# First six up-projection units on six blocks of k, with two modulation groups moved

## The chip, the cores and the metric

One NeuronCore of a Trainium2 chip runs the whole program. The engines named below are TensorE (PE, matrix products; PEld is its weight load), VectorE (DVE), ScalarE (ACT) and SyncE (SP, which here issues nearly all loads). The metric is the device time of one execution in microseconds; three runs of the kernel before are given by their median.

## The reference

One layer of a hybrid decoder on x of 256 tokens by D = 2048, with a conditioning vector c of 2048. All in fp32:

```
mod = silu(c) @ w_ada + b_ada            # 6 rows of 2048: shift, scale, gate twice
h = rms_norm(x) * (1 + scale_m) + shift_m
proj = h @ w_in                          # attention heads and a state-space mixer from it
mix = concat(rms_norm(attn), ssm) @ w_out
x = x + gate_m * mix
h = rms_norm(x) * (1 + scale_f) + shift_f
u = causal_conv3(h @ w_up)               # w_up: 2048 x 11264
x = x + gate_f * ((silu(g) * val) @ w_down)   # g, val: the halves of u
return rms_norm(x)
```

The change concerns the end of the product with w_out, the second norm with its shift and scale, and the product with w_up.

## The kernel before

**Layout.** Features lie on the 128 partitions, tokens along the free axis, so x is 16 blocks (kt) of 128x256. A product goes over the 16 blocks of k. Every weight block is used three times (`mm3`): the rounded weights h times the rounded activations (L277), h times the activations' remainder (L278), and the weights' remainder l times the rounded activations (L279), each 128x128 by 128x256.

**A unit** is a load of mostly 1024 KB (128x2048 fp32, 16 blocks) into a slot of the weight pool. `load_unit` (L252) issues it on SP, `hi_lo_part` makes h by a cast on ACT (L258) and l by a subtraction on DVE (L259), in pieces of 1024 columns. There are four buffers each for h and l, three accumulators in PSUM, and three slots for the loads; during the second half of the out projection three further slots (`wsb`) exist, on memory that the mixer leaves (among it `sqa`, so the first loads into them wait for PE's `ssg`). A slot is free for the next load when the last subtraction (or modulation operation) has read it. SP issues its loads in order: one whose slot is taken holds back all behind it.

**Modulation.** `mod` is made in 24 groups of four units, 1024 KB each (L201). A group in `ON_PE` is done by PE: four products `adp` per unit (L217), and after the fourth unit a row copy on ACT (L221), four column products `adc` (L224) and two small copies on DVE. A group outside it is four DVE operations with an accumulated sum (L210). Groups 12 to 19 give shift and scale of the second norm, two blocks each: 12 to 15 for blocks 0 to 7, 16 to 19 for 8 to 15; 20 to 23 give the last gate.

**Order.** `ORDER` is a list of tokens that the builder follows: `O.h.i` is unit i of half h of the out projection, `ada.g.i` a modulation unit, `N` and `NG` the norm of the mixer's output. A scheduler then places the instructions on the engines; some tokens have a higher priority. The out projection takes first the attention's eight blocks (half 0, `cat`), then the state space's (half 1, `cats`). Between them the second normalisation of the mixer stands: DVE sums squares in `sqa`, PE adds them over the partitions (`ssg`, L623), ACT takes the root (`std_ssm`), DVE the reciprocal (`rs_ssm`, L300), and DVE multiplies (`sn`, L628); ACT rounds the product into `cats`, DVE makes its remainder (L308).

**The feed-forward part** starts with `stats`: PE adds the squares of x over the partitions (`ssx`, L604 to L606), then root and reciprocal (`rs_x`). `h2_gen(a, b)` norms the blocks a to b (per block DVE L312, ACT L313, DVE L314). The product with w_up has 44 pairs of columns; pairs 0 to 21 go in two passes: pass one, `u1a`, takes blocks 0 to 7 of k, one unit of 16 weight blocks for each pair, and is copied out as `part` (L777); pass two, `u2a`, takes blocks 8 to 15 and adds the part. The first two units of pass one (`lead`) are loaded, and the first half of each is split, before the norm is there. Between the units of pass one stand modulation units of groups 17 to 19 on DVE. `w_dn` and the other 22 pairs (`ua`) follow. Below, `s_`, `h_`, `l_` are the load, the rounded part and the remainder of a weight; `o` belongs to w_out, `u` to w_up, `d` to w_dn.

## Time and profile before

| what | value |
| --- | --- |
| three runs | 1196.82, 1199.82, 1199.87 us (median 1199.82) |
| the profiled execution | 1196.57 us, of which the profile's span is 1194.8 |
| PE busy | 1167.5 us, 98% of the span |
| DVE busy | 915.0 us, 77% |
| ACT busy | 636.9 us, 53% |
| out projection, second half | 405.44 to 454.0 us of the span |
| entry of the feed-forward part | 454.03 (first `ssx`) to 460.09 us (first up matmul) |
| up units 2 and 6 of pass one begin | 474.45 and 496.21 us |
| pass two begins | 583.25 us |

Times in the rows are counted from the span's start. A row of a timeline may hold several instructions that follow one another (x2, x3). What stands in brackets behind it is the idle time of the engine just before and what ended it. Neighbouring matmuls overlap, so a matmul costs less than the length of its row.

### The profile page before, as it was taken

How to read it: one execution, taken by the hardware profiler on the slowest of the kernel's cores; microseconds unless marked ns; L12 is line 12 of the kernel's file. 1: busy time of each engine (PE TensorE's matmuls, PEld its weight loads, DVE VectorE, ACT ScalarE, POOL GpSimd, SP SyncE). 2: the span in 40 equal slices, each digit the busy share in tenths (PEclk: the TensorE clock that was granted, in tenths of full speed). 3: DMA queues.
4: the chain of work that ended last, by engine and by line, in shares of the span. 5: the costliest groups of instructions: out<-in, count | busy, mean ns of one | idle time of the engine just before them, and what ended most of it. 6: DMA issues, size and time to landing. Idle time of an engine off the chain costs nothing.

```text
span 1194.8 us, 23406 instructions
## 1 busy us (share of the span) xinstructions
PE 1167.5 (98%) x9760; PEld 1113.3 (93%) x9760; DVE 915.0 (77%) x1371; ACT 636.9 (53%) x959; POOL 0.9 (0%) x7
## 2 busy tenths in 40 slices
PE   6999999999999999999999999999999999999996
PEld 3899989988878898999999999999999999999995
DVE  6889979987988798786599984446888889656554
ACT  4544434457786544446567654444555555555552
POOL 0000000000000000000000000000000000000000
PEclk8899999999999999999999999999999999999998
DMA  9989988776765996997565545558878776545552
GB/s 359 409 338 337 327 335 304 276 268 246 287 242 214 365 383 237 343 357 245 183 204 186 201 146 194 195 194 276 295 299 301 284 282 227 196 150 196 194 194 96
DMA packets 47444, 309.60 MB, mean 259 GB/s; under 512 B 5568, under 2 KB 6761, under 8 KB 16105
## 3 DMA queue, kind: packets, MB, share of 16 engines
q1 hardware_dynamic: 46170, 307.04, 70.6%
q8 instruction: 76, 1.25, 0.4%
q10 hardware_dynamic: 1168, 1.06, 0.4%
q14 instruction: 30, 0.25, 0.1%
HBM read 305.98 MB, written 2.11 MB: 258 GB/s over the span
## 4 chain that ended last, share of the span: by engine, by line
PE 96%; DVE 1%; DMA 1%; ACT 1%; SPq 0%; issue 0%; DVEq 0%; ACTq 0%
PE ua L278 7%; PE ua L279 7%; PE da L279 7%; PE da L278 7%; PE da L277 7%; PE ua L277 7%; PE wa L277 6%; PE wa L279 6%; PE wa L278 6%; PE va L348 4%; PE u1a L278 3%; PE u1a L279 3%; PE u1a L277 3%; PE u2a L277 3%; PE u2a L279 3%; PE u2a L278 3%
## 5 line engine op out<-in xcount | busy, mean ns | idle before, releaser
L258 ACT CAST h_u<-s_u 128x1024 fp32r<-128x1024 f32 x176 | 183.6, 1050 | 188.3 <-PE ua L278 95.2
L259 DVE TENSOR_TENSOR l_u<-s_u,h_u 128x1024 fp32r<-128x1024 f32 x176 | 213.4, 1223 | 66.6 <-ACT h_u L258 64.6
L277 PE MATMUL ua<-h,h_u 128*128 128x256 f32 x704 | 194.3, 276 | 0.0
L278 PE MATMUL ua<-h,h_u 128*128 128x256 f32 x704 | 194.3, 276 | 0.0
L279 PE MATMUL ua<-h,l_u 128*128 128x256 f32 x704 | 194.3, 276 | 0.0
L279 PE MATMUL da<-g,l_d 128*128 128x256 f32 x704 | 194.3, 276 | 0.0
L278 PE MATMUL da<-g,h_d 128*128 128x256 f32 x704 | 194.3, 276 | 0.0
L277 PE MATMUL da<-g,h_d 128*128 128x256 f32 x704 | 194.1, 276 | 0.0
L259 DVE TENSOR_TENSOR l_d<-s_d,h_d 128x1024 fp32r<-128x1024 f32 (+1 forms) x128 | 108.8, 888 | 83.6 <-ACT h_d L258 83.6
L277 PE MATMUL wa<-hT,h_w 128*128 128x256 f32 x576 | 162.1, 282 | 0.8 <-ACT h_w L258 0.8
L279 PE MATMUL wa<-hT,l_w 128*128 128x256 f32 x576 | 159.8, 279 | 0.0
L278 PE MATMUL wa<-hT,h_w 128*128 128x256 f32 x576 | 159.7, 278 | 0.0
L258 ACT CAST h_d<-s_d 128x1024 fp32r<-128x1024 f32 (+1 forms) x128 | 98.2, 782 | 115.0 <-PE da L278 104.3
L210 DVE SCALAR_TENSOR_TENSOR ada<-ada,cb 128x2048 f32<-128x2048 f32 x60 | 137.2, 2288 | 11.5 <-DMA ada<-w_ada 11.2
L279 PEld LDWEIGHTS da<-g,l_d 128*128 128x128 f32 x704 | 132.2, 188 | 0.0
L277 PEld LDWEIGHTS ua<-h,h_u 128*128 128x128 f32 x704 | 132.2, 188 | 0.0
L278 PEld LDWEIGHTS ua<-h,h_u 128*128 128x128 f32 x704 | 132.2, 188 | 0.0
L279 PEld LDWEIGHTS ua<-h,l_u 128*128 128x128 f32 x704 | 132.2, 188 | 0.0
L278 PEld LDWEIGHTS da<-g,h_d 128*128 128x128 f32 x704 | 132.2, 188 | 0.0
L277 PEld LDWEIGHTS da<-g,h_d 128*128 128x128 f32 x704 | 132.1, 188 | 0.0
L258 ACT CAST h_w<-s_w 128x1024 fp32r<-128x1024 f32 x72 | 73.7, 1048 | 88.3 <-PE wa L278 42.7
L277 PEld LDWEIGHTS wa<-hT,h_w 128*128 128x128 f32 x576 | 108.4, 188 | 11.3 <-ACT h_w L258 3.6
(236 smaller groups left out, 2689.4 us busy)
## 6 DMA issues: line engine op xcount, KB each, us to landing
ada<-w_ada SPq DMA_DIRECT2D x96, 1024.0 KB, 6.1
s_u<-w_up SPq DMA_DIRECT2D x88, 1024.0 KB, 5.0
s_d<-w_dn SPq DMA_DIRECT2D x64, 704.0 KB, 4.1
s_w<-w_in SPq DMA_DIRECT2D x36, 1024.0 KB, 7.1
s_o<-w_out SPq DMA_DIRECT2D x16, 1024.0 KB, 8.3
s_v<-w_vdt SPq DMA_DIRECT2D x8, 1040.0 KB, 6.6
x<-xT SPq DMA_DIRECT2D x4, 512.0 KB, 4.8
outT<-x SPq DMA_DIRECT2D x2, 640.0 KB, 3.0
```

The costliest lines, as they stand in the source:

```text
L210: dve.scalar_tensor_tensor(ws[:, :D], ws[:, :D], 1.0, cb, op0=ALU.mult, op1=ALU.mult, accum_out=mod[:, j:j + 1])
L258: act.copy(wh[:, :m], ws[:, o:o + m])
L259: dve.tensor_sub(wl[:, :m], ws[:, o:o + m], wh[:, :m].bitcast(F32))
L277: pe.matmul(o, whs, a[:, 0:T], start=first, stop=False)
L278: pe.matmul(o, whs, a[:, T:2 * T], start=False, stop=False)
L279: pe.matmul(o, wls, a[:, 0:T], start=False, stop=last)
L348: pe.matmul(va[tt][i][:, :n], lo if st == 2 else hi, (wl if st == 1 else wh)[:, s], start=f and st == 0, stop=l and st == 2)
```

## The change

`ON_PE` loses group 14, which so goes to DVE. Group 15 leaves `ORDER` and becomes the first entry of `ada_rest`, the list of the units that are done in pass one, ahead of groups 17 to 23. Since blocks 6 and 7 of the second norm need group 15, the first six pairs (`NEARLY`) take only blocks 0 to 5 of k in pass one, in units of 12 weight blocks (1536 columns, 768 KB), and blocks 6 to 15 in pass two, in two half units of 10 weight blocks (1280 columns, 640 KB) for each pair. The norm of blocks 0 to 5 is made first, that of 6 and 7 behind unit 3. The two lead units' second halves are split only after the sixth block of the norm on DVE (`issue_after`). Group 16 stays on PE ahead of the lead units. The count of up matmuls stays: 72 of them move from pass one to pass two.

```diff
-ON_PE = {2, 6, 9, 10, 11, 12, 13, 14, 16}
+ON_PE = {2, 6, 9, 10, 11, 12, 13, 16}
+
+NEARLY = 6
+UP1 = [[((j, 44 + j), _k)] for _k0, _j0, _j1 in ((6, 0, 6), (8, 6, 22)) for j in range(_j0, _j1) for _k in [tuple(range(_k0))]]
+UP2 = ([[((c,), tuple(range(6, 16)))] for j in range(6) for c in (j, 44 + j)]
+       + [[((j, 44 + j), tuple(range(8, 16)))] for j in range(6, 22)])
...
-O.1.0 O.1.1 ada.14.2 O.1.2 ada.14.3 O.1.3 ada.15.0 O.1.4 ada.15.1 ada.15.2 O.1.5 O.1.6 ada.15.3 O.1.7
+O.1.0 O.1.1 ada.14.2 O.1.2 ada.14.3 O.1.3 O.1.4 O.1.5 O.1.6 O.1.7
...
         dve.tensor_add(par[:, b:b + n], mod[:, b:b + n], V("b_ada", b, n))
         dve.scalar_tensor_tensor(par[:, b:b + n], par[:, b:b + n], 1.0, V(g, k0, n), op0=ALU.add, op1=ALU.mult)
 
-    ada_next = [[8, 0]]
+    ada_rest = [(g, i) for g in (15, 17, 18, 19, 20, 21, 22, 23) for i in range(4)]
 
     def ada_some(n, last=24):
         for _ in range(n):
-            g, i = ada_next[0]
-            if g < last:
-                ada_unit(g, i)
-                ada_next[0] = [g, i + 1] if i < 3 else [g + 1, 0]
+            if ada_rest and ada_rest[0][0] < last:
+                ada_unit(*ada_rest.pop(0))
 
 
     preloaded = []
...
-        dve.scalar_tensor_tensor(dst[:, T:2 * T], t, s, dst[:, 0:T].bitcast(F32), op0=ALU.add, op1=ALU.subtract)
+        return dve.scalar_tensor_tensor(dst[:, T:2 * T], t, s, dst[:, 0:T].bitcast(F32), op0=ALU.add, op1=ALU.subtract)
...
-        else:
-            ada_next[0] = [g, i + 1] if i < 3 else [g + 1, 0]
...
                 steps[it[0]](*it[1:])
         else:
             steps[it[0]](*it[1:])
+    def up1_src(j):
+        return w_up1a[j] if j < NEARLY else w_up1[j - NEARLY]
+
     for j in range(NLEAD):
-        preloaded.append(load_unit(w_up1[j], 2048, f"u1_{j}"))
+        preloaded.append(load_unit(up1_src(j), 1536, f"u1_{j}"))
     for i in range(4):
         ada_pre[16, i] = ada_load(16, i)
     lead_ws = [preloaded.pop(0) for j in range(NLEAD)]
-    lead_hl = [hi_lo_part(lead_ws[j], 0, 1024, f"u1_{j}") for j in range(NLEAD)]
+    lead_hl = [hi_lo_part(lead_ws[j], 0, 768, f"u1_{j}") for j in range(NLEAD)]
     mixctx.close()
     wst["pat"] = [0]
...
     def h2_gen(a, b):
         ada_params(3, a, b - a, "g_ffn")
         for kt in range(a, b):
-            ada_norm(h2[:, kt, :], kt, rs2, par[:, 64 + kt:65 + kt], par[:, 48 + kt:49 + kt], f"2_{kt}")
+            r = ada_norm(h2[:, kt, :], kt, rs2, par[:, 64 + kt:65 + kt], par[:, 48 + kt:49 + kt], f"2_{kt}")
+        return r
 
     hk = [h2[:, k, :] for k in range(KT)]
...
     def resid_add(i, o, gate):
         dve.scalar_tensor_tensor(x[:, i, :], o, gate, x[:, i, :], op0=ALU.mult, op1=ALU.add)
 
-    h2_gen(0, 8)
+    h2_last = h2_gen(0, 6)
     parts = []
     ws, hl = lead_ws, lead_hl
-    ada_some(4, 17)
+    for i in range(4):
+        ada_unit(16, i)
     lead = [acc_tile(f"u1a{j}") for j in range(NLEAD)]
-    for i in range(8):
+    for i in range(6):
         b = slice(i * P, i * P + P)
         for j in range(NLEAD):
-            mm3(lead[j][:, 0:T], hl[j][0][:, b], hl[j][1][:, b], hk[i], i == 0, i == 7)
+            mm3(lead[j][:, 0:T], hl[j][0][:, b], hl[j][1][:, b], hk[i], i == 0, i == 5)
     for j in range(NLEAD):
-        wh, wl = hi_lo_part(ws[j], 1024, 1024, f"u1_{j}")
-        for i in range(8):
+        with tc.issue_after(h2_last.ins):
+            wh, wl = hi_lo_part(ws[j], 768, 768, f"u1_{j}")
+        for i in range(6):
             b = slice(i * P, i * P + P)
-            mm3(lead[j][:, T:2 * T], wh[:, b], wl[:, b], hk[i], i == 0, i == 7)
+            mm3(lead[j][:, T:2 * T], wh[:, b], wl[:, b], hk[i], i == 0, i == 5)
     for j in range(NHALF):
         if j < NLEAD:
             acc = lead[j]
         else:
-            u = weight_unit(w_up1[j], 2048, f"u1_{j}")
+            n = 6 if j < NEARLY else 8
+            u = weight_unit(up1_src(j), 256 * n, f"u1_{j}")
             acc = acc_tile(f"u1a{j}")
-            gemm_pair(acc, u, 0, hk[:8])
+            gemm_pair(acc, u, 0, hk[:n])
         part = gp.tile([P, 512], F32, tag="g", name=f"part{j}")
         act.copy(part, acc)
         parts.append(part)
-        ada_some((16 * (j + 1)) // 18 - (16 * j) // 18, 20)
+        with tc.issue_after(h2_last.ins):
+            ada_some(1 if j < 4 else (12 * (j - 3)) // 16 - (12 * (j - 4)) // 16, 20)
+            if j == 3:
+                h2_gen(6, 8)
     ada_some(100, 20)
     h2_gen(8, 16)
     for half in range(2):
...
         for jj in range(NHALF):
             j = half * NHALF + jj
             if half == 0:
-                w = weight_unit(w_up1[NHALF + j], 2048, f"u2_{j}")
                 acc = acc_tile(f"u2a{j}")
-                gemm_pair(acc, w, 0, hk[8:])
+                if j < NEARLY:
+                    for s in range(2):
+                        w = weight_unit(w_up1b[2 * j + s], 1280, f"u2_{j}_{s}")
+                        gemm_part(acc[:, s * T:(s + 1) * T], w, hk[6:], True, True)
+                else:
+                    w = weight_unit(w_up1[16 + j - NEARLY], 2048, f"u2_{j}")
+                    gemm_pair(acc, w, 0, hk[8:])
                 dve.tensor_add(parts[j], parts[j], acc)
                 us = [parts[j][:, s * T:(s + 1) * T] for s in range(2)]
             else:
...
-    w_up1 = np.stack([unit([((j, 44 + j), _r(8 * h, 8 * h + 8))], wu) for h in range(2) for j in range(NHALF)])
+    w_up1a = np.stack([unit(e, wu) for e in UP1[:NEARLY]])
+    w_up1 = np.stack([unit(e, wu) for e in UP1[NEARLY:] + UP2[2 * NEARLY:]])
+    w_up1b = np.stack([unit(e, wu) for e in UP2[:2 * NEARLY]])
```

The order on DVE from the end of the first half of the out projection to the second's first weights, before (`l1024_o0_7` is the remainder of half 0's last unit, `sqs6` and `sqs7` the last squares):

```order
L259 TENSOR_TENSOR l1024_o0_7_4465<-s_o0_7_4458,h1024_o0_7_4464 128x1024
L617 TENSOR_TENSOR sqa_2378<-sqa_2378,sqs6_4377 128x256
L617 TENSOR_TENSOR sqa_2378<-sqa_2378,sqs7_4529 128x256
L651 TENSOR_TENSOR ot_3633<-ot_3633,rs_attn_3550 128x512
L652 TENSOR_TENSOR x_103<-x_103,ot_3633 128x512
L300 RECIPROCAL rs_ssm1_4542<-std_ssm1_4540 128x256
L628 SCALAR_TENSOR_TENSOR sn4_4544<-cxs_173,vec_92,rs_ssm1_4542 128x256
...
L628 SCALAR_TENSOR_TENSOR sn7_4556<-cxs_173,vec_92,rs_ssm1_4542 128x256
L308 TENSOR_TENSOR cats_4038<-sn4_4544,cats_4038 128x256
...
L308 TENSOR_TENSOR cats_4038<-sn6_4552,cats_4038 128x256
L259 TENSOR_TENSOR l0_o1_0_4568<-s_o1_0_4565,h0_o1_0_4567 128x1024
```

and now (`ada14_0` to `ada14_3` are the units of group 14):

```order
L263 TENSOR_TENSOR l1024_o0_7_4465<-s_o0_7_4458,h1024_o0_7_4464 128x1024
L621 TENSOR_TENSOR sqa_2378<-sqa_2378,sqs6_4377 128x256
L216 SCALAR_TENSOR_TENSOR ada14_0_4521,mod_99<-ada14_0_4521,cb_95 128x2048
L621 TENSOR_TENSOR sqa_2378<-sqa_2378,sqs7_4525 128x256
L216 SCALAR_TENSOR_TENSOR ada14_1_4528,mod_99<-ada14_1_4528,cb_95 128x2048
...
L304 RECIPROCAL rs_ssm1_4535<-std_ssm1_4533 128x256
L216 SCALAR_TENSOR_TENSOR ada14_3_4761,mod_99<-ada14_3_4761,cb_95 128x2048
L632 SCALAR_TENSOR_TENSOR sn4_4537<-cxs_173,vec_92,rs_ssm1_4535 128x256
...
L632 SCALAR_TENSOR_TENSOR sn7_4549<-cxs_173,vec_92,rs_ssm1_4535 128x256
L655 TENSOR_TENSOR ot_3633<-ot_3633,rs_attn_3550 128x512
...
L312 TENSOR_TENSOR cats_4038<-sn7_4549,cats_4038 128x256
L263 TENSOR_TENSOR l0_o1_0_4561<-s_o1_0_4558,h0_o1_0_4560 128x1024
```

Units 0 and 1 of group 14 have come in around the last `sqa` sum, unit 3 ahead of `sn4`, and `l0_o1_0` stands behind all four `cats`, `ot`, `x` and the two `par` operations.

PE at the entry of the feed-forward part, before (`adp16` and `adc16` are group 16's products, `u1a0` and `u1a1` the two lead units):

```order
L604 MATMUL ssx_5160<-sqx_156,ones_96 128x256
L217 MATMUL adp16_5204<-ada16_0_5135,c32_98 32x512 x4
L605 MATMUL ssx_5160<-sq_o14_5126,ones_96 128x256
L606 MATMUL ssx_5160<-sq_o15_5129,ones_96 128x256
L217 MATMUL adp16_5204<-ada16_1_5137,c32_98 32x512 x4
L217 MATMUL adp16_5204<-ada16_2_5139,c32_98 32x512 x4
L217 MATMUL adp16_5204<-ada16_3_5141,c32_98 32x512 x4
L277 MATMUL u1a0_5230<-h2_5159,h0_u1_0_5143 128x256
L277 MATMUL u1a1_5231<-h2_5159,h0_u1_1_5147 128x256
...
L224 MATMUL adc16_5223<-ones_96,row16_5221 128x1 x4
```

and now:

```order
L608 MATMUL ssx_5126<-sqx_156,ones_96 128x256
L223 MATMUL adp16_5162<-ada16_0_5101,c32_98 32x512 x4
L223 MATMUL adp16_5162<-ada16_1_5103,c32_98 32x512 x4
L223 MATMUL adp16_5162<-ada16_2_5105,c32_98 32x512 x4
L223 MATMUL adp16_5162<-ada16_3_5107,c32_98 32x512 x4
L609 MATMUL ssx_5126<-sq_o14_5092,ones_96 128x256
L610 MATMUL ssx_5126<-sq_o15_5095,ones_96 128x256
L230 MATMUL adc16_5181<-ones_96,row16_5179 128x1 x4
L281 MATMUL u1a0_5188<-h2_5125,h0_u1_0_5109 128x256
L281 MATMUL u1a1_5189<-h2_5125,h0_u1_1_5113 128x256
```

The second to fourth unit of group 16 have moved ahead of the last two `ssx`, and `adc16` ahead of the up matmuls.

SP from the last load of group 16 on, before:

```order
L201 DMA ada16_3_5141<-w_ada 128x2048
L201 DMA ada17_0_5340<-w_ada 128x2048
L252 DMA s_u1_2_5343<-w_up1 128x2048
L201 DMA ada17_1_5404<-w_ada 128x2048
L252 DMA s_u1_3_5407<-w_up1 128x2048
L201 DMA ada17_2_5468<-w_ada 128x2048
L252 DMA s_u1_4_5471<-w_up1 128x2048
L201 DMA ada17_3_5532<-w_ada 128x2048
```

and now:

```order
L207 DMA ada16_3_5107<-w_ada 128x2048
L207 DMA ada15_0_5272<-w_ada 128x2048
L207 DMA ada15_1_5277<-w_ada 128x2048
L256 DMA s_u1_2_5280<-w_up1a 128x1536
L207 DMA ada15_2_5329<-w_ada 128x2048
L256 DMA s_u1_3_5332<-w_up1a 128x1536
L207 DMA ada15_3_5381<-w_ada 128x2048
L256 DMA s_u1_4_5395<-w_up1a 128x1536
```

Two loads of group 15 stand ahead of `s_u1_2`; by the slots that they take, `ada15_1` follows the second subtraction of lead unit 0 and `s_u1_2` that of lead unit 1.

## Rows read from the trace of the kernel before

**Rows 1.** The page: busy us, share of span, instructions

```profile
PE 1167.5 (98%) x9760; PEld 1113.3 (93%) x9760; DVE 915.0 (77%) x1371; ACT 636.9 (53%) x959; POOL 0.9 (0%) x7
```

**Rows 2.** Windows: us; busy by engine; granted clock, DMA share, GB/s

```profile
405.44:454.00 48.56, 48.55 (x406) 45.65 (x407) 42.38 (x61) 23.64 (x34) 0.00 (x0) 1.00 0.91 362
...
462.90:466.03 3.13, 3.13 (x16) 3.13 (x16) 3.13 (x7) 0.82 (x2) 0.00 (x0) 0.50 0.56 236
...
474.45:496.21 21.76, 21.76 (x194) 21.76 (x193) 16.20 (x14) 9.08 (x11) 0.00 (x0) 1.00 0.87 332
600.00:700.00 100.00, 100.00 (x885) 100.00 (x884) 95.86 (x168) 70.40 (x112) 0.00 (x0) 1.00 0.54 183
```

**Rows 3.** The page's costliest groups: the modulation on DVE; busy, mean ns, idle before

```profile
L210 DVE SCALAR_TENSOR_TENSOR ada<-ada,cb 128x2048 f32<-128x2048 f32 x60 | 137.2, 2288 | 11.5 <-DMA ada<-w_ada 11.2
```

**Rows 4.** Timeline, DVE, hand-over: start, us, operation, count, idle before

```profile
396.39 0.16 DVE L229 COPY mod<-adc 128x2 f32<-128x2 f32 x1 [1.89 <-PE adc L224]
...
396.53 0.68 DVE L651 TENSOR_TENSOR ot<-ot,rs_attn 128x512 f32<-128x512 f32 x1
...
398.61 1.75 DVE L300 RECIPROCAL rs_ssm<-std_ssm 128x256 f32<-128x256 f32 x1 [0.67 <-ACT std_ssm L298]
400.40 1.67 DVE L628 SCALAR_TENSOR_TENSOR sn<-cxs,vec,rs_ssm 128x256 f32<-128x256 f32 x4
401.99 1.09 DVE L308 TENSOR_TENSOR cats<-sn,cats 128x256 fp32r<-128x256 f32 x3
404.17 1.23 DVE L259 TENSOR_TENSOR l_o<-s_o,h_o 128x1024 fp32r<-128x1024 f32 x1 [1.09 <-ACT h_o L258]
```

**Rows 5.** Timeline of PE at the hand-over

```profile
397.47 0.59 PE L623 MATMUL ssg<-sqa,ones 128*128 128x256 f32 x2
...
402.38 1.92 PE L217 MATMUL adp<-ada,c 128*32 128x512 f32 x16
...
405.44 0.39 PE L279 MATMUL oa<-cats,l_o 128*128 128x256 f32 x1 [0.71 <-DVE l_o L259]
```

**Rows 6.** The page's DMA issues: count, KB each, median us from issue to landing

```profile
ada<-w_ada SPq DMA_DIRECT2D x96, 1024.0 KB, 6.1
...
s_d<-w_dn SPq DMA_DIRECT2D x64, 704.0 KB, 4.1
...
s_o<-w_out SPq DMA_DIRECT2D x16, 1024.0 KB, 8.3
```

**Rows 7.** The chain that ended last, 402 to 430: start us, us, work

```profile
403.09 1.05 ACT h_o L258
...
411.37 0.99 PE adp L217 x6
...
424.59 0.99 PE adp L217 x8
...
428.72 0.79 PE adc L224 x8
```

**Rows 8.** Timeline of PE at the entry of the feed-forward part

```profile
454.03 0.59 PE L604 MATMUL ssx<-sqx,ones 128*128 128x256 f32 x2
454.55 1.06 PE L217 MATMUL adp<-ada,c 128*32 128x512 f32 x8
...
456.61 2.78 PE L217 MATMUL adp<-ada,c 128*32 128x512 f32 x24
460.09 0.51 PE L277 MATMUL u1a<-h,h_u 128*128 128x256 f32 x2 [0.70 <-ACT h L313]
```

**Rows 9.** Timeline of DVE at the entry

```profile
459.01 1.67 DVE L312 SCALAR_TENSOR_TENSOR h<-x,par,rs_x 128x256 f32<-128x256 f32 x4
```

**Rows 10.** Up-unit loads: one issue on SP; issues from 470 to 592

```profile
456.44 0.33 SPq L252 DMA_DIRECT2D s_u<-w_up  x1
...
s_u<-w_up SPq DMA_DIRECT2D x24, 1024.0 KB, 5.4
```

**Rows 11.** What ACT waited for, 470 to 592: us in total, times, longest

```profile
ACT h_u L258 <- DMA s_u<-w_up: 22.2, 11, 4.5
```

More of the change, by code (lines that the diff above doesn't have):

```diff
@@ L94, in hymba_layer @@
 @with_exitstack
-def hymba_layer(ctx, tc, xT, c_row, cT, w_ada, vecs, consts, relb, onehot, w_vdt, w_in, w_out, w_up1, w_up, w_dn, outT):
+def hymba_layer(ctx, tc, xT, c_row, cT, w_ada, vecs, consts, relb, onehot, w_vdt, w_in, w_out, w_up1a, w_up1, w_up1b, w_up, w_dn,
+                outT):
     nc = tc.nc
@@ L895, in _layout @@
         "relb": f(np.concatenate([a["rel_bias"], np.full((1, NH), -1e30, np.float32)], axis=0)),
-        "onehot": oh, "w_vdt": f(w_vdt), "w_in": w_w, "w_out": w_out, "w_up1": w_up1,
+        "onehot": oh, "w_vdt": f(w_vdt), "w_in": w_w, "w_out": w_out, "w_up1a": w_up1a, "w_up1": w_up1, "w_up1b": w_up1b,
         "w_up": w_up, "w_dn": f(w_dn),
     }
-_ORDER = ("xT", "c_row", "cT", "w_ada", "vecs", "consts", "relb", "onehot", "w_vdt", "w_in", "w_out", "w_up1", "w_up", "w_dn")
+_ORDER = ("xT", "c_row", "cT", "w_ada", "vecs", "consts", "relb", "onehot", "w_vdt", "w_in", "w_out", "w_up1a", "w_up1", "w_up1b", "w_up", "w_dn")
 def kernel(**inputs):
```

## The prediction

> **What bounds the kernel now.** I read the page's busy shares and the chain first, then windows, then the timelines of the two places that the change touches. TensorE (PE) is busy for 98% of the span, VectorE (DVE) for 77% [rows 1]; the chain that ended last is nearly all PE. So a PE instruction that goes is worth its own time, unless PE stands still instead, and a transfer or a DVE operation counts only where PE waits for it. The windows [rows 2] say where it doesn't: in the second half of the out projection PE is busy for 48.55 of 48.56 us, in up units 2 to 5 for 21.76 of 21.76, in pass two for 100 of 100. A matmul there costs 21.76/194 = 0.112 us. The two open places are the hand-over from the first half of the out projection (attention, `cat`) to the second (state space, `cats`), where PE waits for `l_o` until 405.44 [rows 5], and the entry of the feed-forward part, 454.03 to 460.09 [rows 8]. The change works on exactly these two, and at both PE's wait is short today because the DVE queue and the weight slots were clear in time.
>
> **The change part by part.** *A, the hand-over.* Group 14 (four DVE operations of 2.288 us [rows 3]) now stands in DVE's queue here: units 0 and 1 around `sqa(7)`, the last sum that `ssg` needs, and unit 3 between the reciprocal `rs_ssm` and `sn`. PE's two `ssg` matmuls stand 20 projection matmuls later than before. In the times of before: `ssg` started at 397.47 and took 0.59 [rows 5]; 20 x 0.112 = 2.24 later it ends at 400.3. DVE is there in time: before, it had idled for 1.89 ahead of the copies at 396.39, and `ot` and `x` ended near 397.9 [rows 4]; less that idle and with two times 2.29 more it is clear at 400.6, and `sqa(7)`, ahead of unit 1, long before. So PE's place decides. From the end of `ssg` (398.06) to the reciprocal (398.61) lie 0.55, and it takes 1.75 [rows 4]: 402.6. Then comes unit 3; its slot is free when unit 0 is through, some four microseconds ahead of 400.6, and with 6.1 for the load [rows 6] it is there by 402.6 or a little sooner: 2.29 more, 404.9. `sn` takes 1.67: 406.6, where before it ended at 402.07. Behind it stand `ot` and `x` (0.68 each, taking `x` as `ot`) and four `cats` (three in 1.09, so 1.45) [rows 4]: 409.4; then `l_o`, 1.23: 410.6. PE's steady run begins at 410.6 and not at 405.44: **+5.2**. The low end is +4.3 (neighbouring DVE rows overlap by up to 0.1, and there are nine). The high end comes from `s_o1_0`, which SP lets go behind `ssg`, as before: 400.3 + 8.3 [rows 6] + a cast of 1.05 [rows 7] = 409.65, a quarter microsecond later than DVE is free: +5.5.
>
> *B, what PE is rid of.* Units 0 and 1 of group 14 ran inside that very wait (1.92 from 402.38 [rows 5]) and give nothing more. Units 2 and 3 lie inside the run without waits: the chain has three rows of them (unit 2 came in two pieces), the first and the last 0.99, the middle one 0.97, and then the group's four column products, 0.79 [rows 7]: **-3.74**. Group 15's four DVE operations and loads leave this run too, which is worth nothing, since PE doesn't wait in it.
>
> *C, the clock.* Behind the entry's wait the trace has a granted clock of 0.50, that is 1.2 GHz, from 462.90 to 466.03 [rows 2]: half of 3.13 us lost, 1.57. Behind the hand-over it is 1.00, for PE's pause was short. Now PE has next to nothing between 402.4 and 410.6, longer than at the entry. I take one such loss, **+1.6**, with ends 0 and 3.1 (the same again at the entry, where I let PE's coming waits hide it).
> The Trainium skill, "TensorE: Matmul & The Clock Gate", Part 1, has the array drop to 1.2 GHz when idle and come back under sustained work. The row at 462.90 agrees. By that rule both pauses would cost, and the term would be 3.1 where nothing hides the second.
>
> *D, from the first `ssx` product to the first up matmul.* Before, one unit of group 16 (1.06) stood between the first `ssx` and the last two, and three (2.78) behind them, hidden by the norm [rows 8]. Now all four stand ahead of the last two. From 454.03 to the end of `ssx` it was 456.61 - 454.03 = 2.58; now it is 0.53 + 1.06 + 2.78 + 1.06 = 5.43. The norm, and with it the first up matmul X (460.09), comes **+2.9** later. The column products of group 16 now lie under the norm instead of between up matmuls; that is in part E.
>
> *E, from X to up unit 6.* Before: 496.21 - 460.09 = 36.1 us [rows 2, 8]. Three weight slots serve this stretch. `s_u1_2` was issued at 456.44 [rows 10], ahead of the norm. Now its slot is freed by the second subtraction of lead unit 1, which must follow six norm blocks on DVE. DVE began the blocks 1.08 ahead of X and takes 0.42 for an operation [rows 9]: 12 of them end at X + 4.0, the two subtractions of 768 columns (0.92 each, three quarters of 1.23) at X + 4.9 and X + 5.8. So `ada15_1` is issued at X + 4.9, `s_u1_2` at X + 5.8. For a landing I take 5.0, between 4.1 for 704 KB [rows 6] and 5.4 for 1024 KB in this stretch [rows 10]. The second unit of group 15 lands at X + 9.9 and holds DVE until X + 12.2; only then comes `l_u` of unit 2, X + 13.4. The 72 lead matmuls, with one microsecond of first waits, end near X + 9.1: PE stands about 4 us. And so on, slot by slot: `s_u1_3` takes that of `ada15_1` (12.2; lands 17.2, cast 18.3, `l_u` 19.5), unit 4 waits on DVE behind `ada15_3` and norm blocks 6 and 7 (24.8), unit 5 follows PE (28.9), unit 6 begins at X + 33.0. The 72 matmuls that moved to pass two cost 72 x 0.112 = 8.1 there. 33.0 + 8.1 - 36.1 = **+5.0**. The same walk with 4.1 a load gives +3.9, with 6.1 it gives +7.2. That loads come last here shows before: ScalarE waited for `s_u` 11 times in this pass, 22.2 us in all [rows 11], with PE just covered.
>
> *F, pass two.* Its first six units have 60 matmuls (6.8 us) instead of 48, and two loads of 640 KB instead of one of 1024. DVE is busy for 95.86 of 100 us there [rows 2], but 512 more columns are 0.6 to 0.7 us for it (half of 1.23, and one more start) against 1.35 us more of PE: nothing, +2 at most if the half units bind each other's buffers.
> A rule that speaks against this part: the Trainium skill, "DMA: Bandwidth & Descriptors", advises in Bandwidth loads of at least 1 MiB, and its Anatomy section gives some 2.0 us of fixed cost for one. The rows agree in direction (704 KB in 4.1 us, not in proportion to 1024 KB in 5.4). By it six more loads are an estimated 12 us of transfer time; were they not hidden, the sum would be +23.
>
> **Sum.** 5.2 - 3.74 + 1.6 + 2.9 + 5.0 = +10.9 (rounded down from 10.96). Against the profiled execution's 1196.57 that is 1207.5. The median of the three runs, 1199.82, lies 3.25 above the profiled one, and the time asked for is a median of such runs: **1210.7**. The bounds: 4.3 - 3.74 + 0 + 2.9 + 3.9 = +7.4, 1204.0 on the profiled time; 5.5 - 3.74 + 3.1 + 2.9 + 7.2 + 2 = +17.0, 1216.8 on the median.
>
> **The rivals.** *One, faster:* both stalls fall away. The point is whether DVE takes `l_o` as soon as its load and cast are there, and whether unit 2's load is off before X. At the quickest landing of [rows 6], 4.1, `l_o` could be ready at 400.3 + 4.1 + 1.05 + 1.23 = 406.7: A is +1.3. With unit 2 in time, E is 216 + 72 matmuls and one microsecond, 288 x 0.112 + 1.1 - 36.1 = -2.7. With C at 0: 1.3 - 3.74 + 2.9 - 2.7 = -2.2, which is 1194.3 on the profiled time and beyond 0.3% against the median only if the runs lie near that one. For it: DVE's 77%. Against it: the queue is in order, and unit 3 stands ahead of `sn` in it. *Two, the same:* A at its low end, no clock loss, and the loads of 768 KB early enough that PE waits as much as before in E (0): 4.3 - 3.74 + 2.9 = +3.5, 1200.0 to 1203.3. Against it: 4.1 us for 704 KB already gives +3.9. *Three, far slower:* loads near 6.1, clock lost twice, half units that bind: 1216.8, and more with the later units of the pass thrown out of step. For it: ScalarE's 22.2 us. That the change doesn't do what it says is no rival here: the order shows PE's group 14 gone and the up matmuls moved.
>
> **How the numbers follow.** Forecast 0.64, rival one 0.06, two 0.12, three 0.18. Faster by over 0.3% (3.6 us, about what a measurement of this kernel can tell from no change): 0.06; within: 0.12; slower: 0.82. The range has my bounds and all of rival two, and ends at 1217, so that rival one and some two thirds of three, 0.18, are left out: 1200 to 1217.
>
> **What would show it.** In the profile after: PE's wait for `oa` in the hand-over, 0.71 before, grown by several microseconds, with DVE or ScalarE as releaser; `ssg` some 2 us later; the first `u1a` 9 us behind the first `ssx`, not 6.06; a wait of some 4 us at unit 2 and shorter ones at units 3 and 4; PE steady from unit 6 on and in pass two. I am wrong if PE is on `cats` by 407, if unit 2 begins without a wait, or if pass two's first six units take clearly more than 6.8 us each.

## The result and the profile after

The changed kernel takes 1209.74 us (median of 4 runs, 1208.36 to 1211.79) against 1198.32 us (4 runs) for the kernel before: the ratio is 1.0097, interval 1.0078 to 1.0116. It is 11.4 us slower; +10.9 was forecast, and the 1210.7 of the prediction is 1.0 too high. The two profiled executions lie 14.3 us apart (1210.84 and 1196.57; spans 1209.1 and 1194.8), since one was above its median and the other below.

The chain that ended last and PE's list of waits in the changed kernel (us in total, times, longest):

```profile
PE 90%; DMA 4%; DVE 4%; ACT 1%; issue 1%; SPq 0%; DVEq 0%; ACTq 0%
...
PE oa L281 <- ACT h_o L262: 5.7, 1, 5.7
PE u1a L283 <- DVE l_u L263: 3.5, 5, 0.9
PE u1a L281 <- ACT h_u L262: 3.1, 2, 1.7
PE u1a L281 <- ACT h L317: 2.6, 1, 2.6
PE oa L283 <- DVE l_o L263: 1.2, 1, 1.2
```

PE was nearly all of the chain before. Now DMA and DVE hold 4% each, and the waits stand where the prediction looked for them: at the hand-over (`oa`), at the norm (`h`), and in pass one (`h_u`, `l_u`).

The stretches of the changed kernel, as windows (us; busy of PE, PEld, DVE, ACT, POOL with counts; granted clock, DMA share, GB/s): from the last `cat` matmul to the first with `l_o`, to `ssx`, to the first up matmul X, to the first down matmul:

```profile
400.94:408.96 8.02, 1.07 (x5) 0.58 (x4) 8.02 (x17) 5.04 (x9) 0.00 (x0) 0.84 0.98 399
408.96:454.32 45.36, 45.36 (x382) 45.36 (x383) 33.20 (x47) 21.09 (x32) 0.00 (x0) 0.95 0.61 227
454.32:462.95 8.63, 6.01 (x48) 2.85 (x46) 3.74 (x8) 3.11 (x7) 0.00 (x0) 1.00 0.33 122
462.95:717.32 254.37, 247.17 (x2113) 245.54 (x2114) 213.69 (x313) 145.54 (x220) 0.00 (x0) 0.98 0.70 250
```

The same stretches in the kernel before, two of them as rows of its trace:

```profile
402.17:405.44 3.27, 2.57 (x21) 0.80 (x19) 2.18 (x5) 2.35 (x5) 0.00 (x0) 1.00 1.03 433
...
460.09:702.93 242.84, 242.30 (x2120) 242.09 (x2121) 201.34 (x292) 144.51 (x209) 0.00 (x0) 0.99 0.68 241
```

The other two were 48.59 and 6.06 us. So the differences are +4.75 (hand-over), -3.23 (second half), +2.57 (entry) and +11.53 (both up passes). From the first down matmul to PE's last matmul, the final norm's, it is 480.2 us in both. The sum is +15.6; 1.2 of it is absent from the spans, because the changed kernel's profiled execution reached the last `cat` matmul 1.2 us earlier (400.94, not 402.17). That belongs to the execution and not to the change: two kernels below, which are the kernel before but for one edit behind that point, reached it at 400.69 and 400.36.

The hand-over on DVE in the changed kernel (start, us, operation, count, idle before):

```profile
394.82 0.42 DVE L621 TENSOR_TENSOR sqa<-sqa,sqs 128x256 f32<-128x256 f32 x1
...
399.58 1.75 DVE L304 RECIPROCAL rs_ssm<-std_ssm 128x256 f32<-128x256 f32 x1 [0.67 <-ACT std_ssm L302]
401.25 2.23 DVE L216 SCALAR_TENSOR_TENSOR ada<-ada,cb 128x2048 f32<-128x2048 f32 x1
403.41 1.67 DVE L632 SCALAR_TENSOR_TENSOR sn<-cxs,vec,rs_ssm 128x256 f32<-128x256 f32 x4
...
407.69 4.62 DVE L263 TENSOR_TENSOR l_o<-s_o,h_o 128x1024 fp32r<-128x1024 f32 x4
```

It is the walk of the prediction, step for step: the reciprocal behind `ssg`, unit 3 of group 14 between it and `sn`, `l_o` last. Its row in [rows 4] began at 404.17. But PE's list names ScalarE for most of the wait: 5.7 us of it end with `h_o`, the cast of the second half's first weights, and only 1.2 with `l_o`. The load of these weights on SP, the casts, and PE's two waits:

```profile
399.07 0.33 SPq L256 DMA_DIRECT2D s_o<-w_out  x1
...
405.86 2.00 ACT L262 CAST h_o<-s_o 128x1024 fp32r<-128x1024 f32 x2 [0.35 <-DMA s_o<-w_out]
...
406.96 0.58 PE L281 MATMUL oa<-cats,h_o 128*128 128x256 f32 x1 [5.74 <-ACT h_o L262]
...
408.96 0.58 PE L283 MATMUL oa<-cats,l_o 128*128 128x256 f32 x1 [1.21 <-DVE l_o L263]
```

The load goes when `ssg` is through, 1.9 us ahead of the last `cat` matmul (4.1 ahead before: 398.10), and lands in some 6.7 us (4.9 before). With a free DVE `l_o` would still have ended near 408.1 (an estimate: the first cast ends at 406.91, `l_o` takes 1.23). So the late load and DVE's queue come out within 0.8 us of each other, as the upper bound of the prediction's part A had it. The move of group 14 is behind both (in e1 below the load goes 4.1 us ahead again), and no run separates them.

PE idles (1.07 us busy of 8.02), and the clock falls. Three windows of the changed kernel, the first right behind the hand-over, the second in the lead units, the third in up unit 2:

```profile
408.96:413.17 4.21, 4.21 (x19) 4.21 (x20) 4.21 (x4) 1.38 (x2) 0.00 (x0) 0.50 0.99 385
...
464.50:467.70 3.20, 3.20 (x17) 3.20 (x16) 3.02 (x7) 1.02 (x2) 0.00 (x0) 0.50 0.00 0
...
478.00:481.40 3.40, 3.40 (x18) 3.40 (x17) 2.00 (x3) 0.09 (x1) 0.00 (x0) 0.50 0.87 276
```

Each is at 1.2 GHz and loses half its length. The second shows more: the DMA share is 0.00. In the first 4.8 us of the lead units next to no weight is under way (0.01 from 462.95 to 467.80). Before, the window from 460.09 to 462.90 had a DMA share of 1.01. The reason is on SP's timeline: the load of unit 2 goes at 468.79, X + 5.84 (X + 5.8 was forecast), where [rows 10] have it 3.65 ahead of X.

```profile
468.79 0.33 SPq L256 DMA_DIRECT2D s_u<-w_up1a  x1
```

The page's two new kinds of load (count, KB each, median us from issue to landing):

```profile
s_u<-w_up1b SPq DMA_DIRECT2D x12, 640.0 KB, 3.8
s_u<-w_up1a SPq DMA_DIRECT2D x6, 768.0 KB, 6.0
```

Behind unit 5, where the prediction's walk ended, the waits go on. Here are unit 6, the gap behind it, and the first half of unit 7:

```profile
497.40:503.10 5.70, 5.67 (x49) 5.46 (x47) 3.36 (x3) 0.59 (x1) 0.00 (x0) 1.00 0.90 348
503.10:505.70 2.60, 0.50 (x2) 0.30 (x2) 1.20 (x2) 2.27 (x3) 0.00 (x0) 0.92 0.62 176
...
505.70:508.90 3.20, 3.12 (x15) 3.12 (x16) 3.20 (x3) 0.20 (x1) 0.00 (x0) 0.53 0.78 251
```

Unit 7's weights come 2.1 us late, and its matmuls then run at 0.53 for 3.20 us.

### The profile page after: what moved, and what is told of

Read it like the earlier page. It is cut to its first block, busy times and chain, and to the rows that moved or that the text cites. A ratio compares the mean times of both kernels' runs of the same rounds, so it can differ in the third digit from the quotient of the medians.

```text
span 1209.1 us, 23396 instructions
## 1 busy us (share of the span) xinstructions
PE 1167.7 (97%) x9720; PEld 1116.8 (92%) x9720; DVE 923.6 (76%) x1392; ACT 636.3 (53%) x970; POOL 0.9 (0%) x7
## 4 chain that ended last, share of the span: by engine, by line
PE 90%; DMA 4%; DVE 4%; ACT 1%; issue 1%; SPq 0%; DVEq 0%; ACTq 0%
PE ua L282 7%; PE ua L281 7%; PE da L281 7%; PE da L282 7%; PE da L283 7%; PE ua L283 7%; PE wa L281 5%; PE wa L283 5%; PE wa L282 5%; PE va L352 4%; PE u2a L283 4%; PE u2a L282 4%; PE u2a L281 4%; PE adp L223 3%; PE oa L281 3%; PE oa L283 3%
## 5 line engine op out<-in xcount | busy, mean ns | idle before, releaser
L262 ACT CAST h_u<-s_u 128x1024 fp32r<-128x1024 f32 (+3 forms) x188 | 184.0, 994 | 165.6 <-PE ua L282 65.4
L263 DVE TENSOR_TENSOR l_u<-s_u,h_u 128x1024 fp32r<-128x1024 f32 (+3 forms) x188 | 212.6, 1152 | 49.4 <-ACT h_u L262 47.4
L216 DVE SCALAR_TENSOR_TENSOR ada<-ada,cb 128x2048 f32<-128x2048 f32 x64 | 146.2, 2286 | 23.9 <-DMA ada<-w_ada 23.3
```

Source lines behind the costliest of these rows:

```text
L216: dve.scalar_tensor_tensor(ws[:, :D], ws[:, :D], 1.0, cb, op0=ALU.mult, op1=ALU.mult, accum_out=mod[:, j:j + 1])
L262: act.copy(wh[:, :m], ws[:, o:o + m])
L263: dve.tensor_sub(wl[:, :m], ws[:, o:o + m], wh[:, :m].bitcast(F32))
```

## The experiments

All times are medians. The kernel before was run beside them on the same chip (1197.72 for e1 to e4, 1197.38 for e5 to e8, 1198.58 for e9 to e11), and the third column gives the difference from that. With four runs its interval is 2 to 3 us to either side. The stretches come from one execution each. They are those above: last `cat` matmul to `ssx`, `ssx` to X, X to the first down matmul.

| kernel | us | over before | to `ssx` | to X | up passes |
| --- | --- | --- | --- | --- | --- |
| before | 1198.32 | - | 51.86 | 6.06 | 242.84 |
| changed | 1209.74 | +11.42 | 53.38 | 8.63 | 254.37 |
| e1, group 14 on PE | 1210.18 | +12.46 | 51.82 | 8.64 | 256.81 |
| e2, group 14 later | 1205.62 | +7.90 | 48.59 | 8.64 | 251.66 |
| e3, split free | 1207.14 | +9.42 | 53.52 | 8.63 | 249.98 |
| e4, `ssx` first | 1207.99 | +10.27 | 53.35 | 6.98 | 253.15 |
| e5, pause filled | 1207.95 | +10.57 | 53.08 | 8.63 | 251.30 |
| e6, before, bound split | 1198.14 | +0.76 | 51.66 | 6.07 | 245.75 |
| e7, group 15 later | 1210.72 | +13.34 | 53.48 | 8.64 | 252.20 |
| e8, e2 + e3 + e4 + e7 | 1197.61 | +0.23 | 47.04 | 6.98 | 245.22 |
| e9, changed, five slots | 1200.15 | +1.57 | 54.07 | 8.64 | 242.73 |
| e10, e8 with five slots | 1191.81 | -6.77 | 48.39 | 6.98 | 240.88 |
| e11, before, five slots | 1196.49 | -2.09 | 51.71 | 6.06 | 243.37 |

**e1: group 14 back on PE.**

```diff
-ON_PE = {2, 6, 9, 10, 11, 12, 13, 16}
+ON_PE = {2, 6, 9, 10, 11, 12, 13, 14, 16}
```

> The changed kernel with group 14 back on PE. Theory: group 14 on DVE costs more at the hand-over than PE gains. In the profile after, PE goes steadily over to the second half 4.8 us later than before, counted from the end of the first half, half a clock for 4.2 us follows (2.1 us lost), and PE is rid of 3.74: a net loss of about 3 us. So this kernel should be about 3 us faster than the changed one, near 1206.6, with the wait of oa for l_o back near 0.7 us and a granted clock of 1.00 behind it. Rival: the hand-over and PE's gain cancel, and the whole loss lies at the entry: then within 1 us of the changed kernel.

The window from the first `l_o` matmul to `ssx`, and, from the chain of the kernel before, PE behind four products of group 14:

```profile
403.93:452.52 48.59, 48.59 (x406) 45.69 (x407) 32.81 (x52) 22.74 (x34) 0.00 (x0) 1.00 0.69 265
...
411.37 0.99 PE adp L217 x6
412.36 0.32 PE oa L279
412.67 0.12 PE oa L277
```

The hand-over is back at 3.23 us, the clock at 1.00, the second half at 48.59, as before. The move of group 14 thus costs 53.38 - 51.82 = 1.6 us net, not 3. In the run's time nothing of it is seen, and by that number the rival held: this execution's up passes were 2.4 us longer. The six kernels with the changed kernel's three slots and its bound split lie between 251.3 and 256.8 there, so a single execution doesn't settle 2 us.

**e2: group 14 on DVE, but in the second half.**

```diff
-... O.0.7 ada.14.0 N.7 ada.14.1 NG.1 close2
-O.1.0 O.1.1 ada.14.2 O.1.2 ada.14.3 O.1.3 O.1.4 O.1.5 O.1.6 O.1.7
+... O.0.7 N.7 NG.1 close2
+O.1.0 O.1.1 O.1.2 O.1.3 ada.14.0 O.1.4 ada.14.1 ada.14.2 O.1.5 O.1.6 ada.14.3 O.1.7
```

> The changed kernel with group 14 still on DVE, but its four units placed between units 3 and 7 of the projection's second half, where group 15 stood before. Theory: the place is what costs, not the engine; DVE has the room there (it was 42.38 of 48.56 us busy with group 15's four units in it). The hand-over should go as before apart from the 1.85 us of group 14 that filled PE's wait, so the end of the second half comes 5 us earlier than in the changed kernel, 7 with the half clock gone: 1203 to 1205. Rival: four DVE operations and loads in that stretch make PE wait there instead: no more than 2 us gained.

PE's wait, the second half as a window, the clock behind the wait, and DVE ahead of its end:

```profile
PE oa L282 <- DVE cats L312: 3.0, 1, 3.0
...
400.51:448.76 48.25, 45.23 (x384) 45.03 (x383) 40.47 (x63) 22.81 (x37) 0.00 (x0) 0.96 0.78 290
...
407.40:410.80 3.40, 3.40 (x18) 3.40 (x18) 1.83 (x2) 0.63 (x1) 0.00 (x0) 0.50 1.02 426
...
400.42 1.66 DVE L632 SCALAR_TENSOR_TENSOR sn<-cxs,vec,rs_ssm 128x256 f32<-128x256 f32 x4
402.00 2.28 DVE L216 SCALAR_TENSOR_TENSOR ada<-ada,cb 128x2048 f32<-128x2048 f32 x1
...
404.21 1.22 DVE L263 TENSOR_TENSOR l_o<-s_o,h_o 128x1024 fp32r<-128x1024 f32 x1
405.35 0.68 DVE L655 TENSOR_TENSOR ot<-ot,rs_attn 128x512 f32<-128x512 f32 x1
405.95 1.42 DVE L312 TENSOR_TENSOR cats<-sn,cats 128x256 fp32r<-128x256 f32 x4
```

`ssx` comes 4.8 us sooner than in the changed kernel and 3.2 sooner than with group 14 on PE. The engine was right, the place wrong. The runs stay just above the 1203 to 1205 that were expected, since the half clock isn't gone (1.7 us from 407.40 to 410.80) and a wait of 3.0 has come. It is DVE's queue again: one unit of group 14 still stands between `sn` and `cats`, with an `l_o` and `ot`, where in [rows 4] `cats` follow `sn` at once. ScalarE had rounded `cats` by 403.37. So even here the place isn't the best one.

**e3: the lead units' second halves split as soon as loaded.**

```diff
-        with tc.issue_after(h2_last.ins):
-            wh, wl = hi_lo_part(ws[j], 768, 768, f"u1_{j}")
+        wh, wl = hi_lo_part(ws[j], 768, 768, f"u1_{j}")
```

> The changed kernel without the rule that the second halves of the two lead units are split only after the sixth norm block. Theory: that rule frees the weight slots late, so that up unit 2 is loaded behind the norm. Without it the load of unit 2 starts before the first up matmul, PE's waits at unit 2 (1.7 and 0.8 us behind a stretch of shorter gaps) go, and the up pass begins pass two 4 to 6 us earlier: near 1205. Rival: three slots and two loads for a unit set the pace whatever the first one does: the wait only moves to units 3 to 5, and less than 1.5 us is gained.

Unit 2's load on SP and the entry as a window:

```profile
458.61 0.33 SPq L256 DMA_DIRECT2D s_u<-w_up1a  x1
...
454.39:463.02 8.63, 6.01 (x48) 2.85 (x46) 4.61 (x9) 3.12 (x7) 0.00 (x0) 1.00 0.87 336
```

The load goes 4.4 us ahead of X, at the entry the DMA share is 0.87 and not 0.33, and PE no longer waits at unit 2. The up passes take 4.4 us less; the runs lie 9.4 us above their kernel before, not 11.4. So the late first slot is one part of the loss. 7 us of it stay, with waits of 1.4 us at unit 3, 0.8 at unit 4 and 1.7 at unit 7: each side of the expectation has a part of it.

**e4: units 1 to 3 of group 16 behind the last `ssx`.**

```diff
-        pe.matmul(ps[:, 0:T], ones, late_sq[1], start=False, stop=True)
+        box["ssx"] = pe.matmul(ps[:, 0:T], ones, late_sq[1], start=False, stop=True)
...
-    for i in range(4):
-        ada_unit(16, i)
+    ada_unit(16, 0)
+    with tc.issue_after(box["ssx"].ins):
+        for i in range(1, 4):
+            ada_unit(16, i)
```

> The changed kernel with units 1 to 3 of group 16 behind the last ssx product, as the kernel before had them. Theory: 2.6 to 2.9 us of products then lie under the norm again. The first up matmul comes 1.5 to 2.5 us earlier after the first ssx (not all 2.9, since the four column products now wait for ScalarE's row copy ahead of the up matmuls): near 1207.5. Rival: the time is given back at unit 2, whose load waits for DVE and not for PE: but DVE's norm blocks move with ssx, so 0.5 us or less gained would speak for it.

The entry takes 6.98 us instead of 8.63, as expected: the cause of term D is shown by the stretch. The runs follow with 10.3 us over their kernel before, not 11.4. The rest of the 2.57 is the column products, now ahead of X, which wait 0.7 us for the row copy.

**e5: PE's pause filled.**

```diff
-        pe.matmul(o, wls, a[:, 0:T], start=False, stop=last)
+        box["mm"] = pe.matmul(o, wls, a[:, 0:T], start=False, stop=last)
...
+        if it == ("O", 1, 0):
+            wt = aux_tile("warm")
+            with tc.issue_after(box["mm"].ins):
+                for q in range(44):
+                    pe.matmul(wt[:, 0:T], ones_r, cat[7][:, 0:T], start=True, stop=True)
```

> The changed kernel with 44 products into an unread accumulator behind the last product of the projection's first half, so that PE works through most of its wait at the hand-over (it leaves nothing of the computation out). Theory: the granted clock of 0.50 from 408.96 to 413.17 follows from PE's pause; with the pause filled it stays at 1.00, the run of the second half is 2.1 us shorter, and nothing else moves: about 1207.6. Rival: the clock falls there for another reason (the weights' transfers, the projection itself): still 0.50, and the time as in the changed kernel or 0.5 us longer for the products.

The filled pause, the end of the hand-over, and what follows:

```profile
400.74:406.23 5.49, 5.49 (x47) 5.29 (x45) 5.49 (x12) 2.49 (x7) 0.00 (x0) 1.00 0.96 372
406.23:409.90 3.67, 1.65 (x11) 1.44 (x12) 3.67 (x7) 3.19 (x4) 0.00 (x0) 1.00 1.01 422
409.90:413.60 3.70, 3.70 (x21) 3.70 (x20) 3.70 (x3) 1.73 (x2) 0.00 (x0) 0.54 0.98 379
```

The theory failed. The long pause was gone, and the clock fell all the same, behind two waits of 1.0 us each (`h_o`, `l_o`) that the products didn't reach. The second half gained 0.3 us, not 2.1. So it doesn't take a long pause; what decides stays open, and the rival's other reasons aren't shown either. The runs lie 10.6 us above their kernel before, 0.9 nearer than the changed kernel; the stretch that was edited accounts for 0.3, the rest is within the scatter of the up passes.

**e6: the kernel before with the bound split alone.**

```diff
...
-    h2_gen(0, 8)
+    h2_last = h2_gen(0, 8)
...
-        wh, wl = hi_lo_part(ws[j], 1024, 1024, f"u1_{j}")
+        with tc.issue_after(h2_last.ins):
+            wh, wl = hi_lo_part(ws[j], 1024, 1024, f"u1_{j}")
```

> The kernel before with one line of the change alone: the second halves of the two lead units are split only after the last (here the eighth) norm block. Theory: the load of up unit 2 starts some 12 us later, behind the norm, instead of 3.65 ahead of the first up matmul, lands near X + 13.5 where PE needs it at X + 14.4, and its cast and subtraction end about 1.5 to 2.5 us late; the three slots then carry the delay on to the next units. 2 to 4 us slower than before: 1200 to 1202. Rival: with 96 lead matmuls instead of 72 PE covers it: within 1 us of before, and then the shorter lead units, and not the late slots, make the wait in the changed kernel.

The ratio is 1.0009, interval 0.9999 to 1.0019: the rival, by its number. In the profile the up passes are 2.9 us longer, in the medians next to nothing is left. But the edit didn't make unit 2's load late, as its row on SP shows:

```profile
456.06 0.33 SPq L252 DMA_DIRECT2D s_u<-w_up  x1
```

That is 2.4 us ahead of X (458.42), 1.3 later than before and not 12. It took the slot that PE's `adp` of group 16 had just left. So the run doesn't test a late load of unit 2. It shows that the bound split alone doesn't make one: in the changed kernel two units of group 15 stand ahead of `s_u1_2` and not one of group 17, and so `s_u1_2` gets the slot of a lead unit.

**e7: group 15 from unit 2 on, groups 17 to 19 spread.**

```diff
-            ada_some(1 if j < 4 else (12 * (j - 3)) // 16 - (12 * (j - 4)) // 16, 20)
-            if j == 3:
+            ada_some(0 if j < 2 else 1 if j < 6 else (12 * (j - 5)) // 14 - (12 * (j - 6)) // 14, 20)
+            if j == 5:
```

> The changed kernel with group 15's units placed at up units 2 to 5 instead of 0 to 3, norm blocks 6 and 7 behind unit 5, and the twelve units of groups 17 to 19 spread over the units from 6 on. Theory of late slots: unit 2's load then takes an earlier slot, its wait is gone, but units 4 to 6 wait instead because the same ten loads go through three slots in the same time: 1 us better at most at unit 6, and 2 to 4 us better in the rest of pass one if the loads there set PE's pace. Rival: the order of the loads is the cause, and moving group 15 back takes all of the 5 us away at unit 6.

Unit 2's load on SP, and PE at unit 4:

```profile
458.87 0.33 SPq L256 DMA_DIRECT2D s_u<-w_up1a  x1
...
484.70 0.38 PE L281 MATMUL u1a<-h,h_u 128*128 128x256 f32 x1 [2.39 <-ACT h_u L262]
485.96 0.58 PE L283 MATMUL u1a<-h,l_u 128*128 128x256 f32 x1 [0.76 <-DVE l_u L263]
```

The load goes 4.4 us ahead of X although the split is still bound, and units 2 and 3 don't wait. Instead unit 4 does, by 3.2 us, and unit 6 begins at X + 33.6 against X + 34.3: the theory of late slots, to its "1 us better at most". In the runs there is no gain, 1210.72. The order of the loads alone isn't the cause.

**e8: e2, e3, e4 and e7 together.**

> The changed kernel with four edits together: group 14 between units 3 and 7 of the second half, lead units split freely, units 1 to 3 of group 16 behind ssx, group 15 from unit 2 on. If the parts simply add (4.1, 2.6 and 1.8 us were gained by the first three), it comes to 1201; if pass one is paced by its loads, an even spread of the modulation units gives 2 to 5 us more, since DMA then never stands still at the entry: 1196 to 1199. Rival: the gains overlap, because all wait for the same three slots: 1203 or more.

1197.61, ratio 1.0000 (0.9976 to 1.0023): the whole loss is back. That is 6.4 us more than the four parts add up to, each against its own kernel before (3.5, 2.0, 1.2 and -1.9). Its runs scatter from 1191.8 to 1201.9.

**e9 and e11: two more slots in the up passes**, in the changed kernel and in the kernel before, on memory that the first down sums take later.

```diff
-            return wst["p"].tile([P, WU], F32, tag="wsa", name=name)
+            return wst["p"].tile([P, wst.get("w", WU)], F32, tag="wsa", name=name)
...
+    fctx = ExitStack()
+    wst.update(p=fctx.enter_context(tc.tile_pool(name="wsf", bufs=2)), pat=[1, 1, 0, 0, 0], i=0, w=D)
...
-    d0 = fp.tile([P, KT, T], F32, name="d0")
...
+        if half == 0:
+            fctx.close()
+            wst["pat"] = [0]
+            d0 = mkpool("d0").tile([P, KT, T], F32, name="d0")
```

> The changed kernel with two more weight slots in the two up passes (memory that the down projection's first sums take later): five instead of three, nothing else changed. Theory: in the changed kernel the stretch from the first up matmul to the first down matmul is 254.4 us against 242.8 before, because each load waits for the subtraction or modulation operation that frees one of three slots, and each wait is followed by a stretch at a granted clock of 0.50. With five slots the loads of units 2 to 7 start ahead of PE's need: 245 to 248 us for the stretch, most of the 11 us back, about 1202. Rival, bytes: the stretch asks for more than the transfers give (two loads in 4.1 to 5.4 us of PE time), so the waits stay with any number of slots: above 251 us, within 3 us of the changed kernel.

> The kernel before with the same two slots in the up passes. Theory: PE is covered there from unit 2 on (21.76 of 21.76 us), so that more slots give nothing: within 1.5 us of before. Rival: the kernel before too loses time to late slots that its profile doesn't show in every execution: 1.5 to 4 us faster.

In e9, unit 2's load on SP, PE from 475 to 500 as a window, and the up passes:

```profile
459.55 0.37 SPq L256 DMA_DIRECT2D s_u<-w_up1a  x1
...
475.00:500.00 25.00, 25.00 (x220) 25.00 (x219) 24.13 (x30) 14.62 (x20) 0.00 (x0) 1.00 1.01 417
...
463.91:706.64 242.73, 242.48 (x2112) 242.19 (x2113) 212.58 (x313) 145.57 (x220) 0.00 (x0) 0.99 0.71 260
```

The load of unit 2 goes 4.4 us ahead of X, PE is busy for 25.00 of 25.00 us, and the transfers bring 417 GB/s meanwhile. The up passes take 242.73 us, 11.6 less than in the changed kernel, as much as before and below the 245 to 248 that were expected: 1200.15 us (1.0010, interval 0.9991 to 1.0028), with order, sizes and places of the changed kernel. So the rival of the bytes falls: the transfers can bring what the stretch asks for, three slots couldn't ask for it in time. An early load of unit 2 isn't enough for that: e3 and e7 had it at the same 4.4 us ahead of X, with three slots, and their up passes took 250.0 and 252.2. In e11 the same slots are worth 2.1 us (0.9978, interval 0.9962 to 0.9994), where at most 1.5 was expected; its profiled execution shows no shorter up passes (243.37), so where they come from is open.

**e10: the four edits and five slots.**

> The kernel of the four edits (group 14 later, split free, ssx first, group 15 from unit 2) with five slots in the up passes. Theory: its hand-over and entry as in the four edits (47 and 7.0 us), the up stretch near 243 instead of 245.2 and without the clock's fall, so the scatter of its executions, 1192 to 1202 before, closes towards the lower end: 1192 to 1195, 2 to 5 us below the kernel before. Rival: the slots don't bind there any more, since it already has hardly a wait: as the four edits alone, 1197.6.

1191.81 us, ratio 0.9928 (0.9909 to 0.9948): faster than the kernel before and than the changed one, with runs from 1189.8 to 1192.2. Its up passes:

```profile
456.17:697.05 240.88, 239.87 (x2115) 239.67 (x2114) 210.28 (x311) 145.38 (x219) 0.00 (x0) 1.00 0.71 260
```

The granted clock is 1.00 throughout them, PE waits once (1.0 us), and the scatter of e8 is gone. The hand-over and second half took 48.39 us and not the expected 47, since the clock fell there (0.96); the up passes made up for it.

## Why the prediction was right, point by point

The total came within a microsecond, and the sign and the two places held. Two terms were mis-sized, in opposite directions: B and E.

- **A, hand-over**: +5.2 forecast, +4.75 measured (8.02 against 3.27), within the bounds. DVE's rows go as forecast, and e1 and e2 undo the loss. But the late load alone would have cost all but 0.8 us of it (an estimate, above). The prediction had this path as its upper bound.
- **B, PE rid of group 14**: -3.74 forecast. The second half became 3.23 shorter although its clock took 2.1 away: -5.3. Only the products' own time in the chain had been counted. Missing are the first projection matmul behind each of them (0.32 instead of 0.12 in the chain of before) and a slower pace of the others: their starts lie 0.115 to 0.118 us apart from 405 to 435 before, and 0.113 from 435 on, as in the changed kernel from 413 on.
- **C, clock**: +1.6 forecast, 2.1 measured at the hand-over (half of 4.21). The Trainium skill, "TensorE: Matmul & The Clock Gate", Part 1, has the array drop to 1.2 GHz when idle. The rows at 408.96 and 464.50 agree: another 1.6 at the second. That one was meant to hide in PE's coming waits, and it does: unit 2's weights are late anyway. The kernel before has the same loss there [rows 2], so it was no difference to begin with. But two of the waits in pass one brought a loss of their own (478.00 and 505.70), which no term had.
- **D, entry**: +2.9 forecast, +2.57 measured, and e4 shows the cause.
- **E, pass one**: +5.0 forecast, +11.5 measured for both passes. The walk itself held up to unit 6: unit 2's `l_u` matmul at X + 13.9 (13.4 forecast), unit 6 at X + 34.3 (33.0), with landings of 6.0 us in the median where it took 5.0. The step that failed is "PE steady from unit 6 on". Of the 6.5 us that were missed, 1.3 lie ahead of unit 6. Behind it come 2.1 of waiting and 1.6 of clock at unit 7 and 0.3 at unit 8; the last 1.2 are spread thin and not assigned. What the runs show in its place: with three slots each load goes only when one clears, and no lead is built up. An early load of unit 2 moves the waits to later units (e3, e7), two more slots end them (e9). The prediction ended its walk where the rows of before are steady, but there the units were longer and the load of unit 2 had gone 9.5 us earlier. How much too small E was is less sure than that it was: the six executions lie 8.5 to 14.0 us above the kernel before, all beyond E's own upper end of 7.2.
- **F, pass two**: nothing forecast beyond the moved matmuls; from the first matmul of pass two to the first down matmul it is 119.7 before and 127.8 now, 8.1 more, which are the 72 matmuls. PE doesn't wait in that stretch, and the loads of 640 KB landed in 3.8 us. The Trainium skill, "DMA: Bandwidth & Descriptors", Bandwidth, advises loads of at least 1 MiB; the smaller ones cost PE nothing here. The 2.0 us of fixed cost that the prediction took from its Anatomy section stand there for loads that GpSimd issues; these go by SP.
- **The base**: the profiled executions differ by 14.3, the medians by 11.4. A to D were together 1.9 too high (5.96 against 4.09), E was 6.5 too low, so against this one execution (15.6 by the stretches) the sum fell short by 4.7, three tenths. That it meets the medians within a microsecond is largely luck: two errors of opposite sign, and a pair of profiled executions that lie 2.9 us further apart than the medians.

Of the rivals, the first (free for PE) has no support: e2 shows that it needs another place, and even there DVE's queue kept PE waiting. The third, loads that set the pace, was half right: PE did wait for loads beyond unit 6, but for want of slots and not of bytes.

## What to carry to other kernels

Before an operation moves to an idler engine, look at that engine's queue at the spot where it will stand: the same four operations cost 1.6 us ahead of a norm and gained 3.2 a few units later. Where few buffers feed a pipeline that runs just even with its consumer, a wait that is taken away at one unit comes back at a later one, so follow the loads to the end of the stretch, and before reordering them ask whether dead memory can hold one or two more buffers. Look in the trace whether an edit moved what it was meant to move before its time is read: e6 didn't. Sum medians with medians: six executions with the same three slots differed by up to 5.5 us in the up passes alone.

## What was not expected of the hardware

- The granted clock fell to 0.54 in e5 behind waits of 1.0 us, although PE had been busy for the 5.5 us ahead of them. In e2 and e10 the second half's window shows 0.96 behind a wait of 3.0 us, in e8 with the same wait 1.00. The kernel before kept 1.00 behind 0.7 us, and the changed kernel behind the waits of 0.8 and 0.9 us at up units 3 and 4. What decides it was not found.
- Matmuls of one shape at a granted clock of 1.00 started up to 0.118 us apart in one stretch of the kernel before and 0.113 in the rest. The DMA share isn't the cause alone: e1 has 0.69 there and the same 48.59 us, the kernel before 0.90. All four kernels with group 14 on PE (before, e1, e6, e11) have the slow stretch from 410 to 435; the changed kernel, e2 and e8, with group 14 on DVE, start theirs 0.113 apart from 415 on. Why stays open.
- With five slots the loads ran at 417 GB/s for 25 us beside a fully busy PE.
